# A mixture-of-experts trunk: the first half's conditional block moved ahead of its gate/up product, and two rooms refilled in quarters

## The chip, the cores and the metric

The kernel runs on one core of one Trainium2 chip. The metric is device time in microseconds; lower is better. The kernel before took 1186.21 us, the median of three runs (1185.47 to 1189.15). The engines are TensorE (PE), ScalarE (ACT), VectorE (DVE), GpSimd (POOL) and SyncE (SP, which here only issues transfers).

## The reference, cut to what matters

Two layers over 256 tokens of width 1024. Each layer is an attention with a residual (layer 0 differential attention, layer 1 latent attention), then a mixture of 64 experts in 8 groups; each token uses the best two experts of its best group.

```
for i in range(2):
    h = rms_norm(x, attn_norm[i])
    x = x + (diff_attention, mla_attention)[i](h, ...)
    h = rms_norm(x, ffn_norm[i])
    x = x + hier_moe(h, ...)

def hier_moe(t):                       # 256 tokens
    combine = ...                      # top group, then top 2 of its 8 experts; 256 x 64 weights
    for e in range(64):
        hid = silu(t @ w_gate[e]) * (t @ w_up[e])        # 1024 -> 256
        acc += combine[:, e, None] * (hid @ w_down[e])   # 256 -> 1024
```

All numbers are float32. Gate, up and down of one expert are 1 MB each, so each layer reads 192 MB of expert weights.

## The kernel before, in words

**Halves.** The experts are taken four at a time: 16 "halves" per layer, t = 0 to 15 (`for t in range(LAST + 1)` in `moe`). Each expert of a half has 32 slots for tokens, so a half is one 128-row tile. For each half: the tokens are gathered into the slots by a product with a 0/1 matrix (`Gather`, L1264, `sel`), gained into `xg` on DVE (L330), multiplied by gate and up of the four experts (`into`, `gate_up`, L1317: 32 matmuls for 8 blocks k of the width and four experts, in four column groups, two trace records each), activated and multiplied (`hidden_rows`: L1325 on ACT, L1327 on DVE), turned (L1335), multiplied by down (L1349), and added back to the token rows `xs` (L1389, L1354).

**Two paths.** If an expert of a half has more than 32 tokens, a second round of 32 slots (`second`) is run for that half. That is decided at run time: `ways` (step `fc`) counts tokens and writes a code `path` (L1242); `values_load` (L1482) loads it into a register of each engine at t = 0, and `full` (L1459) is an `If` on bit t. A further `If` within it (L1414) covers more than 64 tokens. All engines go through each such block. Each engine counts its finished work in a semaphore; at the end of the branch that was taken, an instruction per engine raises its count to a common value, so that what follows can wait for one number whichever way was gone. In the trace these are EVENT_SEMAPHORE at L1459.

**Weights.** Ten rooms of 2 MB in SBUF form a ring. A unit is gate and up of one expert, or down of two experts; unit n stands in the room that unit n - 10 left. `free` names the units whose room is done with, and issues on SP, in a fixed order, the loads that have become possible. In half t the gate/up units of its four experts are freed after the product (within `full`, as `done`, so once in each branch), and the two down units after the down product. Each load waits on SP for the last matmul that read its room. Completion of transfers is counted on eight semaphores in rotation, and a transfer also waits for the one eight before it.

**The start of a layer's experts.** The front of `moe` ends with the steps `FG10 FG11 fc fe0 fe1 fw0 fw1 fv`: the last two parts of the first gather (PE), `ways`, the two parts of `xg` (DVE), the weights of the tokens (L1188 to L1197, DVE and ACT), the weighted matrix (L1279, DVE) and the load of the activation table (ACT, L1115). In layer 0, 16 small DVE operations on the rope tables of layer 1 follow (L263 to L266). At t = 0 all ten rooms are full; experts 0, 1, 2 and 3 stand in rooms 0, 1, 2 and 3 in layer 0, in 9, 0, 1 and 4 in layer 1 (`RING`).

Of the kernel before, what the change touches and what calls it, by code (L numbers as in the profile page):

```python
# [54 lines left out]
ROOMS = 10  # L55
# [14 lines left out]
def trunk_kernel(  # L70
# [5 lines left out]
    nc = tc.nc  # L76
# [1211 lines left out]
    def moe(layer, front):  # L1288
# [6 lines left out]
        def free(units):  # L1295

            state["free"] = state["free"] | set(units)
            while order[state["next"]] - ROOMS in state["free"]:
                load_unit(layer, order[state["next"]])
                state["next"] += 1  # L1300

        def weights_of(g, e, n, part):
            return [front.d6 if (x, part) == (6, "d") else
                    half(expert_room(layer, x, part), x % 2) if part == "d" else rooms[expert_room(layer, x, part)]
                    for x in range(8 * g + e, 8 * g + e + n)]
# [62 lines left out]
        def into(t, j):  # L1368
            g, e, _ = halves_of(t)
            return gate_up(lambda k, at: xg[:, k, j, at], weights_of(g, e, 4, "g"))  # L1370
# [76 lines left out]
        state = {"next": 0, "free": set()}  # L1447
        def full(t, path, done):

            mark = dict(state)

            def at_once():

                state.update(mark)
                done()

            with tc.If((path >> t) & 1, preferred_fallthrough_block=True, label=f"full{layer}_{t}") as more:  # L1459
                second(t, at_once)  # L1460
            with more.Else():
                at_once()
                if t < LAST:
                    tc.mark_branch_hint_location(f"full{layer}_{t + 1}", "LikelyTaken", engines=[PE.engine])
# [5 lines left out]
        for t in range(LAST + 1):  # L1470
            g, _, pairs = halves_of(t)
            weight = None
            if t == LAST:
                back(ts, selT[:, (t + 1) % 2])

                weight = small("sums", 1)
                this.weighted(t, sel[:, (t + 1) % 2])
                DVE.tensor_reduce(weight, this.turned(sel[:, (t + 1) % 2]), axis=AX.XY, op=OP.add)
            gu = into(t, t % 2)
            hid = hidden_rows(gu, weight, held[0][:, 512:768])  # L1480
            if t == 0:
                path = nc.values_load(front.path[0:1, 0:1], min_val=0, max_val=2 ** 17 - 1)  # L1482
            full(t, path, lambda: free(units(g, pairs, "gu")))
            if t == LAST:
                rows = temp(256).bitcast(F32R).rearrange("p (b t) -> p b t", b=2)
                hdT = hidden_columns(hid)
# [99 lines left out]
```

## Time and profile before

| what | value |
|---|---|
| median of three runs | 1186.21 us (1185.47 to 1189.15) |
| the profiled execution | 1189.65 us, of which the span of the trace is 1187.9 us |
| PE busy | 970.6 us, 82% of the span |
| DVE, ACT busy | 425.8 us (36%), 232.0 us (20%) |
| mean granted TensorE clock | 0.935 of full speed |
| read from HBM | 433.03 MB |

The profile cuts the span into 40 slices of 29.7 us. Its GB/s line tells where the transfers run at their full pace (some 425) and where they don't; PE's idle time is listed by what ended it. Layer 0's experts begin at about 151 us, layer 1's at about 738 us; the starts of both are read closely below.

### The profile page before, as it was taken

The numbers are of one execution on the slowest core, as the hardware profiler recorded it, in microseconds if no ns is written. First come the engines' busy times: TensorE is split into PE (matmuls) and PEld (weight loads), VectorE is DVE, ScalarE is ACT, GpSimd is POOL, SyncE is SP. The second block draws the span as 40 slices with busy tenths as digits, with TensorE's granted clock in tenths as the row PEclk, the third lists the DMA queues.
The fourth block names the chain that finished last, engine by engine and source line by source line (L and its number), as shares of the span: only waits on it lengthen the run. The fifth ranks groups of instructions, "written<-read, shape, count | busy, mean of one in ns | idle before, by whom it ended". The sixth has DMA issues, their size and how long they took to land. (4 is left out here: it accounts for less than half of the span.)

```text
span 1187.9 us, 16711 instructions
## 1 busy us (share of the span) xinstructions
PE 970.6 (82%) x6544; PEld 544.0 (46%) x6544; DVE 425.8 (36%) x996; ACT 232.0 (20%) x594; POOL 1.3 (0%) x23
## 2 busy tenths in 40 slices
PE   8999888887776777777888999877777777789787
PEld 8897744433332333333448777533333333333343
DVE  6898633221111111111339886222111211113233
ACT  5666410000000000000017874100000000000001
POOL 0000000000000000000000000000000000000000
PEclk9999989998898889988999999989888988899999
DMA  9556968999999999999953387899999999999996
GB/s 353 203 210 261 353 255 363 383 425 426 425 425 425 426 425 425 426 426 426 412 220 141 136 311 300 354 426 425 426 426 426 426 425 426 425 424 378 424 426 263
DMA packets 78013, 435.97 MB, mean 367 GB/s; under 512 B 6960, under 2 KB 23088, under 8 KB 30128
## 3 DMA queue, kind: packets, MB, share of 16 engines
q1 hardware_dynamic: 77728, 434.02, 88.7%
q8 instruction: 86, 1.41, 0.4%
q14 instruction: 55, 0.45, 0.1%
q10 hardware_dynamic: 144, 0.09, 0.0%
HBM read 433.03 MB, written 1.05 MB: 365 GB/s over the span
## 5 line engine op out<-in xcount | busy, mean ns | idle before, releaser
L1317 PE MATMUL bank<-room,areaC 128*32 128x512 f32 x2240 | 332.0, 675 | 105.2 <-DMA room<-in_moe_w_up_dram 105.2
L1317 PEld LDWEIGHTS bank<-room,areaC 128*32 128x32 f32 x2240 | 97.0, 123 | 329.8 <-issue 314.5
L1327 DVE TENSOR_TENSOR prob<-temp,bank 128x256 f32<-128x256 f32 x33 | 13.9, 422 | 385.9 <-ACTq L1459 192.8
L1349 PE MATMUL bank<-room,aT 128*32 128x512 f32 (+1 forms) x1160 | 128.3, 572 | 1.2 <-ACT aT L1337 1.2
L1354 DVE TENSOR_TENSOR xs<-xs,bank 128x512 f32<-128x512 f32 (+1 forms) x148 | 96.9, 659 | 79.2 <-PE bank L1389 74.9
L1389 PE MATMUL bank<-prob,val 128*128 128x512 f32 x240 | 111.3, 607 | 3.1 <-issue 2.0
L1325 ACT ACTIVATE temp<-bank 128x256 f32<-128x256 f32 x35 | 13.4, 384 | 481.7 <-PE bank L1317 481.7
L418 PE MATMUL bank<-room,areaB 128*128 128x256 f32 (+3 forms) x544 | 87.9, 314 | 5.0 <-DVE room L386 2.8
L1264 PE MATMUL bank<-val,areaB 128*128 128x128 f32 x576 | 75.2, 292 | 18.8 <-DVE val L1256 15.2
L330 DVE TENSOR_TENSOR areaC<-bank,pack 128x512 f32<-128x512 f32 x70 | 48.4, 692 | 114.0 <-PE bank L1264 114.0
L1264 PEld LDWEIGHTS bank<-val,areaB 128*128 128x128 f32 x576 | 71.3, 205 | 24.6 <-DVE val L1256 17.4
L418 PEld LDWEIGHTS bank<-room,areaB 128*128 128x128 f32 x544 | 77.3, 194 | 10.0 <-DVE room L386 3.3
L1264 PE MATMUL bank<-val,areaA 128*128 128x128 f32 x544 | 66.9, 282 | 16.3 <-DVE val L1256 13.7
L1264 PEld LDWEIGHTS bank<-val,areaA 128*128 128x128 f32 x544 | 63.6, 196 | 20.5 <-DVE val L1256 17.3
L1389 PEld LDWEIGHTS bank<-prob,val 128*128 128x128 f32 x240 | 44.5, 196 | 50.6 <-issue 49.0
L1349 PEld LDWEIGHTS bank<-room,aT 128*32 128x32 f32 x1160 | 34.5, 109 | 67.4 <-issue 59.4
L386 DVE TENSOR_TENSOR room<-room,room 128x2048 fp32r<-128x2048 f32 (+4 forms) x33 | 62.4, 1898 | 4.3 <-ACT room L384 4.3
L1381 ACT COPY prob<-bank 128x512 f32<-128x512 f32 x30 | 17.6, 586 | 189.0 <-PE bank L1349 189.0
L384 ACT CAST room<-room 128x2048 fp32r<-128x2048 f32 (+4 forms) x33 | 51.8, 1590 | 5.2 <-DMA room<-in_diff_w_in_dram 2.7
L1381 DVE COPY prob<-bank 128x512 f32<-128x512 f32 x30 | 20.8, 692 | 89.4 <-PE bank L1349 89.4
L1285 PE MATMUL bank<-ident,val 128*128 128x128 f32 x74 | 15.5, 292 | 44.8 <-DVEq L1459 28.0
L418 PE MATMUL bank<-room,areaA 128*128 128x512 f32 (+1 forms) x176 | 42.9, 387 | 2.0 <-DVE areaA L688 2.0
(245 smaller groups left out, 734.5 us busy)
## 6 DMA issues: line engine op xcount, KB each, us to landing
room<-in_moe_w_gate_dram SPq DMA_DIRECT2D x124, 1024.0 KB, 19.5
room<-in_moe_w_up_dram SPq DMA_DIRECT2D x124, 1024.0 KB, 19.6
room<-in_moe_w_down_dram SPq DMA_DIRECT2D x122, 1024.0 KB, 19.6
room<-in_diff_w_in_dram SPq DMA_DIRECT2D x11, 1024.0 KB, 10.7
room<-in_diff_w_out_dram SPq DMA_DIRECT2D x2, 2048.0 KB, 9.4
room<-in_moe_w_gate_dram SPq DMA_DIRECT2D x8, 512.0 KB, 14.8
room<-in_moe_w_up_dram SPq DMA_DIRECT2D x8, 512.0 KB, 13.6
room<-in_moe_w_down_dram SPq DMA_DIRECT2D x8, 512.0 KB, 10.0
```

What stands on the lines that cost most here:

```text
L330: DVE.tensor_tensor(dst, tp, gain[:, k0:k0 + n, None].to_broadcast([128, n, dst.shape[2]]), op=OP.mult)
L384: step(c + name)(lambda f=f: f(hi().bitcast(F32R), w()))
L386: step(c + name)(lambda eng=eng: eng.tensor_tensor(lo().bitcast(F32R), w(), hi(), op=OP.subtract))
L418: PE.matmul(out, a[k][x_].bitcast(F32R), b[k][w_].bitcast(F32R), start=first and j == 0, stop=last and j == n - 1)
L1264: PE.matmul(self.ps[kk][:, k, :], self.front.xn[:, tb, 4 * kk + k, :], self.sel[:, tb, :], start=tb + k == 0, stop=tb == 1, skip_group_che ...
L1285: PE.transpose(tp[:, tb, :], (self.sel if sel is None else sel)[:, tb, :], ident)
L1317: PE.matmul(gu[M * c:M * c + M], x(k, slice(M * c, M * c + M)), w[:, :, k, :], start=k == 0, stop=k == 7)
L1327: DVE.tensor_mul(hid, sil, gu[:, 256:512])
L1349: PE.matmul(y[n][M * c:M * c + M], hdT[:, k, M * c:M * c + M], w[:, k, ns], start=first and k == 0, stop=last and k == 1, skip_group_check ...
L1354: DVE.tensor_add(xs[:, tb, ns], xs[:, tb, ns], acc)
L1381: (ACT.copy, DVE.tensor_copy)[n](t, y[n])
L1389: PE.matmul(acc, rows[:, tb, :], t, start=True, stop=True)
```

## The change

At t = 0 the `If` block stands ahead of the first gate/up product and no longer frees anything in its branches. The product follows it. Then `refill(4)` issues the loads that the freed rooms allow: gate and up of experts 7 and 9, which go to the rooms of experts 0 and 2, are cut into four parts along k (256 KB each, 2 KB per partition, where it was 1 MB and 8 KB), part by part for both experts; then down of 7, 8 and 9 in whole, into the rooms of experts 1 and 3. Bytes and rooms are the same. For t = 1 to 15 nothing changes but line numbers. (`load_expert` with `cuts` was there before.)

```
+        def refill(cuts):
+            for c in range(cuts):
+                for e in (7, 9):
+                    load_expert(layer, e, "gu", cuts, c)
+            for n in (ROOMS + 1, ROOMS + 4):
+                load_unit(layer, n)
+            state["next"] = 4
...
+            if t == 0:
+                path = nc.values_load(front.path[0:1, 0:1], min_val=0, max_val=2 ** 17 - 1)
+                full(t, path, lambda: None)
             gu = into(t, t % 2)
             hid = hidden_rows(gu, weight, held[0][:, 512:768])
             if t == 0:
-                path = nc.values_load(front.path[0:1, 0:1], min_val=0, max_val=2 ** 17 - 1)
-            full(t, path, lambda: free(units(g, pairs, "gu")))
+                refill(4)
+                free(units(g, pairs, "gu"))
+            else:
+                full(t, path, lambda: free(units(g, pairs, "gu")))
```

PE in layer 0 before, from the end of the first gather into the first product (rooms 0 to 3 carry numbers of their tiles: room_69, room_1590, room_1523 and room_72; names in brackets are the semaphores waited for, DVE_49 that of DVE, DMAHW those of transfers):

```order
L1264 MATMUL bank<-val,areaB 128x128 [waits DVE_49,Activation_49]
L1264 MATMUL bank<-val,areaB 128x128 x7
L1317 MATMUL bank<-room_69,areaC 32x512 [waits DMAHW1_49,DMAHW5_49,DMAHW0_49,DVE_49]
L1317 MATMUL bank<-room_1590,areaC 32x512 [waits DMAHW4_49,DMAHW3_49]
L1317 MATMUL bank<-room_1523,areaC 32x512 [waits DMAHW2_49,DMAHW1_49]
L1317 MATMUL bank<-room_72,areaC 32x512 [waits DMAHW7_49,DMAHW5_49]
L1317 MATMUL bank<-room_69,areaC 32x512 [waits DMAHW6_49]
```

The product stood right behind the gather; its wait for DVE is for the count that the first part of `xg` gives (302).

PE at the same place now, from the gather into the block:

```order
L1264 MATMUL bank<-val,areaB 128x128 [waits DVE_49,Activation_49]
L1264 MATMUL bank<-val,areaB 128x128 x7
L1490 TENSOR_LOAD path [waits DVE_49]
L1468 REGISTER_ALU
L1468 COMPARE_AND_BRANCH
L1596 BRANCH_PREFETCH_HINT
L1264 MATMUL bank<-val,areaB 128x128 [waits DVE_49,PE_49]
```

The load of `path` and the branch have moved between them; the last row is already the second round, which runs only if its bit is set.

PE now, from the end of the block into the first product:

```order
L1468 UNCONDITIONAL_BRANCH
L1596 BRANCH_PREFETCH_HINT
L1468 UNCONDITIONAL_BRANCH [waits PE_49]
L1326 MATMUL bank<-room_69,areaC 32x512 [waits DMAHW0_49,DMAHW1_49,DVE_49,DMAHW5_49,PE_49,Activation_49]
L1326 MATMUL bank<-room_1590,areaC 32x512 [waits DMAHW4_49,DMAHW3_49]
L1326 MATMUL bank<-room_1523,areaC 32x512 [waits DMAHW2_49,DMAHW1_49]
L1326 MATMUL bank<-room_72,areaC 32x512 [waits DMAHW7_49,DMAHW5_49]
L1326 MATMUL bank<-room_69,areaC 32x512 [waits DMAHW6_49]
```

The product's first matmul now waits for DVE, PE and ACT at once. In the built program the numbers are 354 for DVE and 168 for ACT; ahead of the block's end those counts reach 334 (with the last rope operation) and 150, and the block's end adds 28 and 20. In layer 1 it is 1254 for DVE, where 1238 is reached (with L1279) and 28 are added.

SP in layer 0 before, the loads in the branch that is taken when bit 0 is clear:

```order
L147 DMA room_69<-in_moe_w_gate_dram 128x2048 [waits DMAHW3_49,PE_49]
L147 DMA room_69<-in_moe_w_up_dram 128x2048 [waits DMAHW4_49]
L143 DMA room_1590<-in_moe_w_down_dram 128x2048 [waits DMAHW5_49,PE_49]
L147 DMA room_1523<-in_moe_w_gate_dram 128x2048 [waits DMAHW6_49,PE_49]
L147 DMA room_1523<-in_moe_w_up_dram 128x2048 [waits DMAHW7_49]
L143 DMA room_72<-in_moe_w_down_dram 128x2048 [waits DMAHW0_49,PE_49]
L143 DMA room_72<-in_moe_w_down_dram 128x2048 [waits DMAHW1_49]
```

Seven loads, each of the four rooms released by the last matmul that read it.

SP now, the first two of four parts, behind the block:

```order
L147 DMA room_69<-in_moe_w_gate_dram 128x512 [waits DMAHW3_49,PE_49]
L147 DMA room_69<-in_moe_w_up_dram 128x512 [waits DMAHW4_49]
L147 DMA room_1523<-in_moe_w_gate_dram 128x512 [waits DMAHW5_49,PE_49]
L147 DMA room_1523<-in_moe_w_up_dram 128x512 [waits DMAHW6_49]
L147 DMA room_69<-in_moe_w_gate_dram 128x512 [waits DMAHW7_49,PE_49]
L147 DMA room_69<-in_moe_w_up_dram 128x512 [waits DMAHW0_49]
L147 DMA room_1523<-in_moe_w_gate_dram 128x512 [waits DMAHW1_49,PE_49]
L147 DMA room_1523<-in_moe_w_up_dram 128x512 [waits DMAHW2_49]
```

Sixteen quarter loads and three whole ones stand here now; the first waits for the product's matmuls of k = 0 and 1 alone.

## Rows read from the trace of the kernel before

**Rows 1.** The page: GB/s in 40 slices; the costliest group of PE.

```profile
GB/s 353 203 210 261 353 255 363 383 425 426 425 425 425 426 425 425 426 426 426 412 220 141 136 311 300 354 426 425 426 426 426 426 425 426 425 424 378 424 426 263
...
L1317 PE MATMUL bank<-room,areaC 128*32 128x512 f32 x2240 | 332.0, 675 | 105.2 <-DMA room<-in_moe_w_up_dram 105.2
```

**Rows 2.** Stretches: us; PE, PEld, DVE, ACT, POOL busy; clock, DMA share, GB/s.

```profile
185.00:190.00 5.00, 5.00 (x52) 1.43 (x44) 0.00 (x0) 0.00 (x0) 0.00 (x0) 1.00 0.56 234
...
210.00:215.00 5.00, 5.00 (x52) 1.53 (x48) 1.33 (x3) 0.59 (x1) 0.00 (x0) 1.00 0.59 193
...
215.00:220.00 5.00, 5.00 (x48) 1.30 (x40) 0.00 (x0) 0.00 (x0) 0.00 (x0) 1.00 1.00 418
...
750.00:755.00 5.00, 5.00 (x49) 2.79 (x51) 1.38 (x2) 0.59 (x1) 0.00 (x0) 1.00 1.01 419
```

**Rows 3.** Timeline of layer 0's start: us from start, us taken, what; [idle before].

```profile
148.63 0.15 DVE L1242 CAST path<-temp 128x1 int32<-128x1 f32 x1
...
151.61 7.14 PE L1317 MATMUL bank<-room,areaC 128*32 128x512 f32 x64
...
157.84 0.18 DVE L266 SCALAR_TENSOR_TENSOR sin_t<-pack,pack 128x32 f32<-128x32 f32 x1
...
158.77 0.34 SPq L147 DMA_DIRECT2D room<-in_moe_w_gate_dram  x1
...
160.73 0.41 PE L1285 MATMUL bank<-ident,val 128*128 128x128 f32 x2 [1.98 <-PEq L1459]
...
167.76 3.64 PE L1349 MATMUL bank<-room,aT 128*32 128x512 f32 x32
```

**Rows 4.** Timeline of layer 1's start.

```profile
737.48 0.15 DVE L1242 CAST path<-temp 128x1 int32<-128x1 f32 x1
...
738.65 7.34 PE L1317 MATMUL bank<-room,areaC 128*32 128x512 f32 x64
...
743.01 0.42 DVE L1279 TENSOR_TENSOR val<-val,wt 128x256 f32<-128x256 f32 x1
...
745.74 0.34 SPq L147 DMA_DIRECT2D room<-in_moe_w_gate_dram  x1
```

**Rows 5.** Block at t = 0, layer 0: ns min/median/max, start in us.

```profile
L1459 PEldq COMPARE_BRANCH  x1: 3590/3590/3590, 156.7 to 156.7; - x1
L1482 PEldq TENSOR_LOAD <-path x1: 491/491/491, 156.0 to 156.0; - x1
L1459 DVEq EVENT_SEMAPHORE  x1: 21/21/21, 160.3 to 160.3; - x1
L1482 DVEq TENSOR_LOAD <-path x1: 541/541/541, 159.3 to 159.3; - x1
```

**Rows 6.** The same in layer 1.

```profile
L1459 PEldq COMPARE_BRANCH  x1: 3833/3833/3833, 743.5 to 743.5; - x1
L1482 PEldq TENSOR_LOAD <-path x1: 317/317/317, 743.0 to 743.0; - x1
L1459 DVEq EVENT_SEMAPHORE  x1: 21/21/21, 747.5 to 747.5; - x1
L1482 DVEq TENSOR_LOAD <-path x1: 322/322/322, 746.5 to 746.5; - x1
```

**Rows 7.** Who waited for instructions of L1459: us, times.

```profile
  PE bank L1285: 41.8, 28
```

**Rows 8.** Timeline of PE: the gate/up product behind waits of different lengths.

```profile
351.03 7.03 PE L1317 MATMUL bank<-room,areaC 128*32 128x512 f32 x58 [1.46 <-DMA room<-in_moe_w_up_dram]
...
781.32 4.50 PE L1317 MATMUL bank<-room,areaC 128*32 128x512 f32 x20 [3.84 <-DMA room<-in_moe_w_up_dram]
...
840.36 9.18 PE L1317 MATMUL bank<-room,areaC 128*32 128x512 f32 x58 [3.89 <-DMA room<-in_moe_w_up_dram]
```

**Rows 9.** Stretches: clock behind that wait; transfers in 1 KB pieces (layer 0's attention weights).

```profile
840.00:845.00 5.00, 4.64 (x24) 1.35 (x28) 0.00 (x0) 0.00 (x0) 0.00 (x0) 0.53 1.01 423
...
20.00:30.00 10.00, 10.00 (x86) 10.00 (x84) 8.09 (x34) 5.20 (x7) 0.00 (x0) 1.00 1.09 386
```

**Rows 10.** Timeline of PE: the gather behind a product with no block between.

```profile
179.64 3.84 PE L1264 MATMUL bank<-val,areaB 128*128 128x128 f32 x32 [1.37 <-DVE val L1256]
```

## The prediction

> **What bounds the kernel now.** I read the page first. Its GB/s line stands at about 425 through most of both expert stretches, and PE's largest idle time, 105.2 us at the gate/up product, is ended by transfers [rows 1]. So the experts are paced by the stream of weights, and what counts is when that stream starts and where it stops for want of a free room. Second, the stretches. In layer 0 the stream stops twice more after its start: it is busy for 0.56 of 185 to 190 us and 0.59 of 210 to 215, with PE busy for all of both; from 215 on it is full [rows 2]. Until about 213 us, layer 0 is therefore paced by PE, whose progress frees the rooms. In layer 1 the stream is full from 750 on, and its slices stay at 425 up to the one of 378 near the end [rows 1, 2]; PE comes to that later dip from waits for weights, so I take it to move with the stream. Third, the timelines of the two starts, for what the change moves [rows 3, 4], and the queue instructions of the block [rows 5, 6]. At t = 0 bit 0 is clear in both layers: the trace shows no second round between the first product and the first down product.
>
> This gives two gauges. Layer 0 ends later or earlier by the shift of PE, read at the first down product (now at 167.76, [rows 3]); when its first loads start matters little there, since the stream runs dry at 185 to 190 anyway. Layer 1 moves by the shift of its first load (now at 745.74, [rows 4]).
>
> **The wait that is added.** The first product used to wait for `xg` only. Behind the block it waits for a count that DVE reaches only at the block's end, and DVE gets there behind everything queued ahead: token weights, the weighted matrix and, in layer 0, the 16 rope operations. Before, these lay beside the product, which covered them; that cover is gone. That engines do wait for each other at the block's end is shown: 28 times, 41.8 us in all, PE's next transposes waited for instructions of L1459 [rows 7].
>
> When is DVE through? In layer 0 its last rope operation ends at 157.84 + 0.18 = 158.02, in layer 1 L1279 ends at 743.01 + 0.42 = 743.43 [rows 3, 4]. From the load of `path` to the instruction at the block's end it took 160.3 - 159.3 and 747.5 - 746.5, 1.0 us each [rows 5, 6]. Between nothing of that hidden and all of it, the end falls at 158.0 to 159.0 and 743.4 to 744.4. I let the load start with the last operation: 158.8 and 744.0, and 0.1 us more for PE to see it. The product then starts at 158.9 instead of 151.61, and at 744.1 instead of 738.65. Behind it on PE stand the gather and the first down product; ACT and DVE wait for its result, and SP, at the head of whose queue the refill stands, for its matmuls.
>
> PE's own way through the block is shorter and hidden: `path` is written at 148.78 and 737.63, and from PE's load to the end of its branch it took 156.7 + 3.59 - 156.0 = 4.3 us, and 4.3 in layer 1 [rows 3 to 6], so PE would be through at about 153.1 and 741.9. The Trainium skill ("Runtime: NRT & Kernel Launch", Instruction fetch mechanics) says that a taken branch whose target has not been fetched stalls the sequencer until it is; the 3.59 and 3.83 us of PE's branch agree. If that were all that the block costs here, the time would be that of the rival "PE's own branch" below.
>
> **The clock.** PE is then idle for 7.3 us in layer 0 and 5.5 in layer 1. Behind an idle time of 3.89 us the granted clock was 0.53 in 840 to 845, that is the 1.2 GHz level for nearly all of it, and 58 records of the product took 9.18 us; behind one of 1.46 us the same took 7.03 [rows 8, 9]. I add the difference, 2.15, to the product's 7.14: 9.3 us. Bounds: 7.14, if the clock holds, and 14.3 if it stayed low throughout.
>
> **Layer 0, summed at PE.** Behind the product the block is gone: 1.37 us to the gather, which takes 3.84 [rows 10]. The down product begins at 158.9 + 9.3 + 1.4 + 3.8 = 173.4, against 167.76: +5.7 us. Ends: 158.0 + 7.14 + 5.2 = 170.3, +2.6; 159.1 + 14.3 + 5.2 = 178.6, +10.9. The removed 1.98 us behind the product [rows 3] and whatever slowed the gather there before are in this sum. The loads of experts 7 and 9 start when k = 0 and 1 are done, some 3.6 us into a product at low clock (20 records in 4.50 us, 16 needed, [rows 8]): 162.5, against 158.77. They need 4.2 MB / 0.425 = 9.9 us plus a start of 1 to 2, so they are in by 174; the second product, 3.64 us behind 173.4, takes them at 177. Three microseconds hide them.
>
> **Layer 1, summed at the stream.** First load at 744.1 + 3.6 = 747.7, against 745.74: +2.0. Ends: 743.4 + 1.8 (a quarter of 7.14) = 745.2, -0.5; 744.5 + 3.6 = 748.1, +2.4. The stream then has 7 MB queued (17 us) and must get the two down rooms before 765; the first down product ends at 744.1 + 9.3 + 5.2 + 3.64 = 762.2, in time. Smaller pieces: 1 KB ones ran at 386 GB/s [rows 9], 8 KB ones at 425; 2 KB lie between, so the 4.2 MB cost 0 to 1.0 us more; I take 0.4. The issues are no bound: sixteen at 0.34 us [rows 3, 4] make 5.4 us for 9.9 us of transfer. In layer 0 both are hidden behind PE. Together +2.4.
>
> The Trainium skill ("DMA: Bandwidth & Descriptors", Bandwidth) advises at least 1 MiB per transfer and gives 341 GB/s for 1 MB alone and 138 for 64 KB; by the lower figure the 4.2 MB would take an estimated 30 us, 20 more. The trace has several transfers in flight and 386 GB/s in finer pieces, which speaks against it here.
>
> **Sum.** +5.7 + 2.4 = +8.1 us on the profiled execution (1189.65 us, span 1187.9). That lies 3.4 above the median, without a sign that the two starts differ, so I put the sum on the median: 1186.2 + 8.1 = 1194.3.
>
> **The rivals.**
> 1. *The clock holds* (the idle time falls so that the low level is short): 158.9 + 7.14 + 5.2 - 167.76 = +3.5, and 744.1 + 1.8 - 745.74 = +0.2; 1189.9. For it: behind 1.46 us nothing was lost [rows 8], and the low level ends by itself once PE is busy. Against it: idle times here are longer than the 3.89 that brought the low level.
> 2. *PE's own branch is the only price*, the other side: if the product started at 153.1 and 741.9, layer 0 would be 153.1 + 7.14 + 5.2 - 167.76 = -2.3, layer 1 741.9 + 1.8 - 745.74 + 0.4 = -1.6; 1182.3, faster by 0.33%. It decides if DVE is through the block before 155 and 743. Against it: DVE's rows end at 158.0 and 743.4, and the wait is in PE's rows of the change. Only if the count were met earlier than I read it does this hold.
> 3. *Layer 0's delay is taken up by the stream*: if the loads, not PE, set 213 us, only layer 1's +2.4 is left; 1188.6. For it: 2 us of stream idle at 210 to 215. Against it: that idle time is ended by PE's progress.
> 4. *Quarters starve the stream*: at half the pace the 4.2 MB take 9.9 us more in layer 1, and in layer 0 the second product waits some 7 us: 1211. Against it: the 386 GB/s.
>
> **Chances.** The forecast 0.70 (its own range 1191 to 1198: the block's end by 0.5 us, the clock by 2 us, in both layers); the clock holds 0.13; PE's own branch 0.05; taken up 0.07; quarters 0.05. About 0.3%, 3.6 us, is what a measurement of this kernel can tell from no change: 1182.7 to 1189.8. Rival 1 lies on that edge and is halved. Slower: 0.70 + 0.07 + 0.05 = 0.82; same: 0.06 + 0.07 = 0.13; faster 0.05. The range 1188.5 to 1198.5 leaves out the quarters, PE's own branch and the far end of the clock.
>
> **What would show it.** In the profile after: the first product at about 159 in layer 0 and 744 in layer 1, with PE's idle time before it of 7 and 5.5 us, ended by DVE's or PE's queue at L1468; a clock near half in its first microseconds; the first quarter load at 162 and 747.5; the first down product at 173; then the gap of the stream at 190 to 196 and 216 to 219, as before but 5 to 6 later. A first product at 153 would make me wrong, and so would a layer 0 that reaches full stream at 215 in spite of a late down product.

## The result, and the profile after

The changed kernel takes 1206.4 us (median of 6 runs, 1204.21 to 1210.59); the kernel before took 1188.36 beside it (6 runs, 1185.47 to 1189.52). The ratio is 1.0153, with a 95% interval of 1.0137 to 1.0170: 18 us slower, where 8.1 had been forecast. The profiled execution has a span of 1204.2 us, 16.3 more than the one of before. In this kernel the block's lines are L1468 and L1490, the product L1326, the gather still L1264, the down product L1358.

The page, in the lines that answer to [rows 1]: the stream is paced as before, and PE's idle time ahead of the product has grown from 105.2 to 121.2 us, of which transfers ended 109.0.

```profile
GB/s 354 195 234 255 326 226 266 383 426 426 424 426 425 426 426 426 425 425 426 416 254 141 126 311 297 297 425 425 426 426 425 426 426 426 425 422 360 424 424 258
...
L1326 PE MATMUL bank<-room,areaC 128*32 128x512 f32 x2240 | 330.7, 675 | 121.2 <-DMA room<-in_moe_w_up_dram 109.0
```

The other 12.2 stand in the view of who waited for instructions of L1468 (us, times; answers to [rows 7]): two waits of the product, one in each layer, that the kernel before did not have.

```profile
  PE bank L1326: 12.2, 2
```

Layer 0's start, in the timeline (start, duration, what, idle before; answers to [rows 3, 10]):

```profile
147.81 0.15 DVE L1242 CAST path<-temp 128x1 int32<-128x1 f32 x1
...
157.01 0.19 DVE L266 SCALAR_TENSOR_TENSOR sin_t<-pack,pack 128x32 f32<-128x32 f32 x1
157.47 9.17 PE L1326 MATMUL bank<-room,areaC 128*32 128x512 f32 x64 [6.61 <-DVEq L1468]
161.09 0.34 SPq L147 DMA_DIRECT2D room<-in_moe_w_gate_dram  x1
...
171.79 3.64 PE L1358 MATMUL bank<-room,aT 128*32 128x512 f32 x32
```

Layer 1's start in the same view (answers to [rows 4]):

```profile
746.44 2.02 PE L1264 MATMUL bank<-val,areaA 128*128 128x128 f32 x16 [0.73 <-DVE temp L1237]
...
747.22 0.15 DVE L1242 CAST path<-temp 128x1 int32<-128x1 f32 x1
...
754.05 9.57 PE L1326 MATMUL bank<-room,areaC 128*32 128x512 f32 x64 [5.59 <-DVEq L1468]
757.67 0.34 SPq L147 DMA_DIRECT2D room<-in_moe_w_gate_dram  x1
```

And the block's own instructions in layer 0, as [rows 5] showed them (ns, then start in us):

```profile
L1468 PEldq COMPARE_BRANCH  x1: 3561/3561/3561, 148.8 to 148.8; - x1
L1468 DVEq EVENT_SEMAPHORE  x1: 21/21/21, 157.2 to 157.2; - x1
```

All this is what the prediction described. PE is through its branch at 152.4, and the product waits until DVE, behind its last rope operation, is at the block's end; it then takes 9.2 and 9.6 us, and 155 to 160 us has a granted clock of 0.50 (below), the 1.2 GHz level. What the prediction did not have comes later, on PE, in the second half of the experts (t = 1), which in layer 0 takes a second round (gather, product). Its first product ran as before, from 175.24 for 7.05 us; then:

```profile
183.76 1.80 PE L1264 MATMUL bank<-val,areaB 128*128 128x128 f32 x14 [1.46 <-DVE val L1256]
189.58 4.00 PE L1264 MATMUL bank<-val,areaB 128*128 128x128 f32 x18 [4.02 <-issue]
193.51 8.05 PE L1326 MATMUL bank<-room,areaC 128*32 128x512 f32 x64
```

Before, the same gather ran in one piece of 3.84 us ([rows 10]) and the product behind it took 7.07 from 183.40. Now PE stops for 4.02 us after 14 of the 32 matmuls, waiting for nothing that the profile shows ("issue"), and then runs the rest at a low clock (0.50 in 190 to 195 us). The gather ends 6.0 us later behind its start than before, the product takes 1.0 us more: 7.0 us together. The stretches show what it does to the stream of weights (PE, PEld, DVE, ACT, POOL busy; clock, DMA share, GB/s; answers to [rows 2]):

```profile
155.00:160.00 5.00, 2.53 (x12) 1.67 (x16) 2.17 (x18) 0.22 (x1) 0.00 (x0) 0.50 0.00 0
...
190.00:195.00 5.00, 5.00 (x25) 3.69 (x28) 1.72 (x3) 0.00 (x0) 0.00 (x0) 0.50 0.37 157
195.00:200.00 5.00, 5.00 (x48) 1.40 (x44) 0.00 (x0) 0.00 (x0) 0.00 (x0) 0.95 0.00 0
200.00:205.00 5.00, 3.23 (x32) 1.10 (x28) 0.42 (x1) 1.03 (x3) 0.00 (x0) 1.00 0.51 159
220.00:225.00 5.00, 5.00 (x50) 1.89 (x52) 1.26 (x2) 0.59 (x1) 0.00 (x0) 1.00 0.61 252
```

Before, at the first stop of the stream, the transfers were busy for 0.56 of one slice (185 to 190) and 0.72 of the next; now for 0.37, nothing and 0.51 of three (190 to 205).

**Where the 16.3 us are.** I summed the GB/s column over stretches of 2 us, in this trace and in that of before, and compared the times at which the same number of bytes had arrived. Bytes are counted from 140 us of each execution on, so that its lead or lag at that time is taken out (the changed kernel's was 0.9 us ahead there); the span is as it is. The table (us later than before; every kernel's single profiled execution) is used for the experiments too. Executions differ by themselves: e10, which leaves layer 0 as it was before, shows -1.4 there, so a difference of 1 to 2 us in one cell proves nothing. 10 MB lies at 177 us of the kernel before, 40 at 255, 210 at 718 (just ahead of layer 1's experts), 240 at 802, 370 at 1111.

| kernel | 10 MB | 40 MB | 210 MB | 240 MB | 370 MB | span |
|---|---|---|---|---|---|---|
| changed | +5.0 | +12.0 | +10.7 | +15.2 | +16.6 | +16.3 |
| e1, no hint in layer 0 | +6.1 | +5.0 | +4.1 | +11.5 | +13.1 | +17.5 |
| e2, hint later | +4.4 | +10.8 | +10.3 | +16.9 | +16.3 | +16.6 |
| e3, whole loads | +7.5 | +11.1 | +10.9 | +21.0 | +22.0 | +23.8 |
| e4, block behind the product | +6.3 | +0.6 | +0.3 | +6.8 | +9.3 | +10.0 |
| e5, DVE early | +1.4 | +7.5 | +6.7 | +8.2 | +8.9 | +9.3 |
| e6, e1 and e5 | +0.9 | +0.7 | -0.1 | +1.6 | +1.9 | +2.5 |
| e7, quarters inside the block | -2.9 | +3.4 | +2.8 | +1.1 | +1.9 | +1.2 |
| e8, halves inside the block | -2.2 | +3.9 | +2.9 | +1.7 | +2.5 | +1.5 |
| e9, PE filled | +7.7 | +6.7 | +13.2 | +23.3 | +24.9 | +26.1 |
| e10, quarters in layer 1 | -1.4 | -1.5 | -1.4 | -3.0 | -1.9 | 0.0 |
| e11, e10 without the hint | -1.5 | -0.1 | 0.0 | -2.7 | -3.4 | -4.0 |
| e12, e9 less one hint | +8.7 | +6.4 | +6.8 | +14.3 | +15.1 | +14.5 |
| e13, quarters backward | +10.4 | +18.2 | +17.3 | +30.0 | +29.7 | +29.9 |

For the changed kernel: 5.0 us for the late first product, 7.0 for the idle time at t = 1 and the low clock behind it, 1.3 given back in the rest of layer 0 and in layer 1's attention, 4.5 at the start of layer 1's experts, 1.4 in layer 1's late stretch; the 1.3 and the 1.4 are no larger than what executions differ by. Of the 4.5, the first load gives little over 2 (it is 11.93 us later than before, `path` 9.74) and the quarters' slow arrival the rest, 2.3.

### The profile page after: what moved, and what is told of

Same layout as the page of the kernel before. It is cut to its first block, busy times and chain, and to the rows that moved or that the text cites. A ratio compares the mean times of both kernels' runs of the same rounds, so it can differ in the third digit from the quotient of the medians.

```text
span 1204.2 us, 16755 instructions
## 1 busy us (share of the span) xinstructions
PE 968.8 (80%) x6544; PEld 544.4 (45%) x6544; DVE 425.3 (35%) x996; ACT 232.0 (19%) x594; POOL 1.3 (0%) x23
## 5 line engine op out<-in xcount | busy, mean ns | idle before, releaser
L1326 PE MATMUL bank<-room,areaC 128*32 128x512 f32 x2240 | 330.7, 675 | 121.2 <-DMA room<-in_moe_w_up_dram 109.0
L1326 PEld LDWEIGHTS bank<-room,areaC 128*32 128x32 f32 x2240 | 99.1, 123 | 342.6 <-issue 327.1
L1358 PE MATMUL bank<-room,aT 128*32 128x512 f32 (+1 forms) x1160 | 128.3, 572 | 1.2 <-ACT aT L1346 1.2
L1264 PE MATMUL bank<-val,areaB 128*128 128x128 f32 x576 | 75.6, 293 | 21.8 <-DVE val L1256 15.1
L1264 PEld LDWEIGHTS bank<-val,areaB 128*128 128x128 f32 x576 | 71.7, 206 | 27.7 <-DVE val L1256 15.1
L1264 PE MATMUL bank<-val,areaA 128*128 128x128 f32 x544 | 66.8, 282 | 16.4 <-DVE val L1256 13.7
L1264 PEld LDWEIGHTS bank<-val,areaA 128*128 128x128 f32 x544 | 63.5, 195 | 20.6 <-DVE val L1256 17.3
L1358 PEld LDWEIGHTS bank<-room,aT 128*32 128x32 f32 x1160 | 34.5, 109 | 67.4 <-issue 59.4
L1285 PE MATMUL bank<-ident,val 128*128 128x128 f32 x74 | 15.1, 285 | 42.0 <-DVEq L1468 26.6
## 6 DMA issues: line engine op xcount, KB each, us to landing
room<-in_diff_w_in_dram SPq DMA_DIRECT2D x11, 1024.0 KB, 10.7
```

Source lines behind the costliest of these rows:

```text
L1264: PE.matmul(self.ps[kk][:, k, :], self.front.xn[:, tb, 4 * kk + k, :], self.sel[:, tb, :], start=tb + k == 0, stop=tb == 1, skip_group_che ...
L1285: PE.transpose(tp[:, tb, :], (self.sel if sel is None else sel)[:, tb, :], ident)
L1326: PE.matmul(gu[M * c:M * c + M], x(k, slice(M * c, M * c + M)), w[:, :, k, :], start=k == 0, stop=k == 7)
L1358: PE.matmul(y[n][M * c:M * c + M], hdT[:, k, M * c:M * c + M], w[:, k, ns], start=first and k == 0, stop=last and k == 1, skip_group_check ...
```

## The experiments

The theories: the late first product costs what the prediction said, and (1) the idle time at t = 1 comes from the branch hint that PE executes as it leaves the block, or from the place of the code, or from both; (2) quarters arrive slowly, by themselves or because of the product beside them. Ratios are to the kernel before, run beside each.

### The hint of the second half (e1, e2)

In the block's `Else`, PE executes a hint that the next half's block will be jumped over. In layer 0 that is wrong for t = 1, which falls through into its second round. e1 leaves this one hint out:

```
             with more.Else():
                 at_once()
-                if t < LAST:
+                if t < LAST and t + layer:
                     tc.mark_branch_hint_location(f"full{layer}_{t + 1}", "LikelyTaken", engines=[PE.engine])
```

> The changed kernel, less one instruction of PE in layer 0: the branch hint for the block of the second half (t=1) that PE executes as it leaves the block of the first half. Theory A (the hint stands in the way of the code that follows in line): the 4.0 us idle in the gather of the second half's second round (14 matmuls, idle, 18 matmuls, at 185.6 to 189.6 us) goes, the clock holds, the product behind it takes 7 instead of 8 us and starts near 187.5 instead of 193.5; the stream's stop at 195 to 200 us goes; time 1206.4 - 7 = 1199.5 us (1198 to 1201). Rival B (the place of the code: the same idle comes from where the moved instructions end a piece of code that is loaded as one): the idle stays where it is, time 1206 us (1205 to 1208). Rival C: the idle goes, but the stream takes the 7 us back before the end of layer 0, time 1206 us with no gap in the trace.

Measured: 1203.18 us, ratio 1.0113 (1.0098 to 1.0128). PE's timeline of it, against the rows of the changed kernel above, and at the end of the front of layer 1:

```profile
184.26 3.81 PE L1264 MATMUL bank<-val,areaB 128*128 128x128 f32 x32 [1.46 <-DVE val L1256]
188.00 7.07 PE L1326 MATMUL bank<-room,areaC 128*32 128x512 f32 x64
...
740.72 3.75 PE L1264 MATMUL bank<-val,areaA 128*128 128x128 f32 x16 [0.73 <-DVE temp L1237]
...
750.05 10.07 PE L1326 MATMUL bank<-room,areaC 128*32 128x512 f32 x64 [5.58 <-DVEq L1468]
```

The idle time is gone, and layer 0's stream is 7.0 us earlier at 40 MB, as A said; C is out. The whole gained some 5 us by the ratios (1.0153 less 1.0113), not 7, and the time missed A's bound of 1201. Where the rest went is not shown. The profiled execution is the slowest of the four (1207.22 us; the others took 1202.37 to 1203.63) and slower than the changed kernel's: its last gather ahead of layer 1's product ran for 3.75 us where that took 2.02, its stream lost 7.4 us there instead of 4.5, and some 4 more behind 370 MB.

e2 gives the hint, but behind the first product:

```
-                if t < LAST:
+                if 0 < t < LAST:
                     tc.mark_branch_hint_location(f"full{layer}_{t + 1}", ...)
...
             if t == 0:
+                tc.mark_branch_hint_location(f"full{layer}_1", "LikelyTaken", engines=[PE.engine])
                 refill(4)
```

> The changed kernel with the branch hint for the second half's block moved from the end of the first block, ahead of the first product, to behind that product, in both layers, as it stands in the order of the kernel before. The run without the hint in layer 0 lost the 4.0 us idle there, so the hint takes part in it. Theory A (what matters is that the hint comes 131 PE instructions ahead of where it was): the idle goes, the time is that of the run without the hint, ratio 1.011 (1203 us). Rival B (the hint does it wherever it stands, together with where the code ends): the 4 us idle stays in the second round's gather, ratio 1.015 (1206 to 1208 us).

Measured: 1210.29 us, ratio 1.0185 (1.0165 to 1.0204). The gather again stops after 14 matmuls: rival B.

```profile
189.10 4.00 PE L1264 MATMUL bank<-val,areaB 128*128 128x128 f32 x18 [4.05 <-issue]
```

So it isn't the order of hint and product, which the kernel before had like this, too. What differs from before is then where the code lies, or when PE comes to it; the runs below speak for the place.

### The code moved by 96 instructions (e9, e12)

e9 puts 48 small matmuls on PE between the block and the first product; they also tell what the low clock costs.

```
                 full(t, path, lambda: None)
+                idle = psum_bank()
+                for _ in range(48):
+                    PE.matmul(idle[:, 0:128], ones_b, ones_b, start=True, stop=True)
             gu = into(t, t % 2)
```

> The changed kernel with 48 dummy matmuls of 128 columns (as the ones that the kernel has at its start) on PE between the block and the first product, in both layers, where PE waits for DVE. They move PE's code behind them by 96 instructions and keep PE busy. Clock (theory A: the product is slow because PE was idle): the first product takes 7.1 to 7.6 us in place of 9.2 to 9.6, starting when it did, layer 1's stream 1.5 us earlier. Code (theory A: 4 us idle comes with the hint wherever a piece of code ends): the idle moves 96 instructions ahead, into the second half's first product, and stays 4 us. Rival B: the place of the code matters too and the idle goes. Time: 1.0153 - 0.002 - 0.001 = 1.012 to 1.013 (1204 us) with the idle kept, 1.007 (1198 us) without it.

Measured: 1213.57 us, ratio 1.0201 (1.0166 to 1.0235). PE's timeline, start and the two second rounds of layer 0:

```profile
156.06 4.62 PE L1494 MATMUL bank<-ones_b 128*128 128x128 bf16 x48 [6.55 <-DVEq L1468]
160.61 7.07 PE L1326 MATMUL bank<-room,areaC 128*32 128x512 f32 x64
...
184.88 3.81 PE L1264 MATMUL bank<-val,areaB 128*128 128x128 f32 x32 [1.46 <-DVE val L1256]
188.62 7.07 PE L1326 MATMUL bank<-room,areaC 128*32 128x512 f32 x64
...
601.69 1.47 PE L1264 MATMUL bank<-val,areaB 128*128 128x128 f32 x11 [1.42 <-DVE val L1256]
607.61 4.85 PE L1264 MATMUL bank<-val,areaB 128*128 128x128 f32 x21 [4.45 <-issue]
```

Three things follow. The dummies waited for DVE's end of the block themselves (the same label, 6.55 us) and so came on top of it, which I had not foreseen; the time says nothing of the clock's worth. But the product behind the busy dummies took 7.07 us instead of 9.17, at a granted clock of 1.00 in 160 to 165 us (0.52 in 155 to 160, where the dummies ran): the 2.1 us were the idle time's. And the stop at t = 1 is gone with its hint in place, while the other second round of layer 0, that of t = 15, has one that neither kernel had: 4.45 us, and 6.5 us lost in the stream between 40 and 210 MB. The expectation's theory A had the stop move into the first product of t = 1; it did not, so that form of the theory falls.

e12 is e9 less the hint for t = 15 in layer 0:

```
-                if t < LAST:
+                if t < LAST and (layer or t != 14):
```

> The run with 48 dummy matmuls lost the 4 us idle at the second half's second round, and got 4.45 us of idle in the gather of the other second round that layer 0 takes, that of the last half (11 matmuls, idle, 21 matmuls, at 603.2 to 607.6 us). Here that run's kernel less the one hint for the last half's block in layer 0. Theory A (a hint for a block that is not jumped over, and a piece of code that ends soon behind it, make the idle): the 4.45 us go, with 0.7 us of slower product behind, ratio 1.0201 - 0.005 = 1.015. Rival B (the idle there belongs to the dummies' shift of the code alone): it stays, ratio 1.020.

Measured: 1206.49 us, ratio 1.0149 (1.0134 to 1.0164), as A had it. The gather of t = 15 in PE's timeline:

```profile
602.15 3.81 PE L1264 MATMUL bank<-val,areaB 128*128 128x128 f32 x32 [1.42 <-DVE val L1256]
605.89 7.07 PE L1326 MATMUL bank<-room,areaC 128*32 128x512 f32 x64
```

So in two places a stop of 4.0 to 4.5 us needed both: a hint for a block that then fell through, and the code at that place. It is the place and not the moment: in e5 below PE comes to this gather 4.5 us earlier and stops behind the same 14 matmuls. What points at code being fetched are the transfers of the changed kernel in 187.0 to 187.5 us, half a microsecond within the stop (queue, packets, MB, share of 16 engines):

```profile
q1 hardware_dynamic: 27, 0.19, 89.3%
q8 instruction: 1, 0.02, 12.0%
```

One packet of 0.02 MB of instructions lies in it, between weights that fill the engines. In 146 to 196 us the changed kernel has four such packets (near 149.5, 153, 172.5, 187), e1 five. Read in steps of 0.1 us, every stop of this kind has one (changed, e2, e3, e5, e9, e13, and the shorter stops within a gather of the kernel before, e4, e10 and e11), and PE goes on 2.2 to 2.5 us behind it. But e1 has a packet at the same point of the gather, 3.5 us behind its start, and no stop, so a packet alone doesn't make one. That the hint takes the place of the piece that follows in line is the reading that fits; which piece each packet brought the trace does not say, so this mechanism is argued, and only the parts of the hint and of the place are shown.

The Trainium skill ("Runtime: NRT & Kernel Launch", Instruction fetch mechanics) calls the prefetch purely sequential and names the taken branch as what breaks it. Here the stop stood behind a branch that was not taken, but hinted as taken (4.02 us, none without the hint); the page has no such case.

### DVE's work behind the product (e5), and with e1 (e6)

e5 leaves ahead of the block only what ACT's exponentials need; the rest of the token weights, the weighted matrix and the rope tables come behind the first product.

```
-            step("fv")(lambda: (self.first.weighted(0), ACT.preload_act_table_set("silu_and_others")))
+            step("fv")(lambda: ACT.preload_act_table_set("silu_and_others"))
...
             ACT.activation(e2, d, AF.Exp)
+
+        def weights_end(self, tb):
             DVE.scalar_tensor_tensor(se, e2, 1.0, sg, op0=OP.add, op1=OP.mult)
...
             gu = into(t, t % 2)
+            if t == 0:
+                for tb in range(2):
+                    front.weights_end(tb)
+                this.weighted(0)
+                if layer == 0:
+                    for tb in range(2):
+                        rope_tables(1, tb)
```

> The changed kernel with DVE's work on the token weights (behind their exponentials), the weighted rows and the rope tables put behind the first product in the program, so that DVE comes to the end of the block some 4.5 us earlier in layer 0 and 3.4 us in layer 1. Theory A (the product waits for DVE's queue at the end of the block, as its idle of 6.61 and 5.59 us is labelled): product of layer 0 starts at 153.0 instead of 157.5 and of layer 1 3.4 us earlier after the path (3.4 instead of 6.8 us behind it); if PE's clock holds over the shorter wait each takes 7.2 instead of 9.2 to 9.6 us. Layer 1's first load comes 4 to 5 us earlier behind the path. Time 1206.4 - 4.4 - 4.4 = 1197.6 us (1195 to 1201) with the idle at the second round staying. Rival B (PE itself, by its taken branch, is what comes last): product starts within 1 us of where it did, time 1206 us.

Measured: 1201.22 us, ratio 1.0100 (1.0083 to 1.0117). The timeline, both layers:

```profile
148.22 0.15 DVE L1246 CAST path<-temp 128x1 int32<-128x1 f32 x1
...
153.30 8.82 PE L1328 MATMUL bank<-room,areaC 128*32 128x512 f32 x64 [3.75 <-DVE wt L1201]
...
743.34 0.15 DVE L1246 CAST path<-temp 128x1 int32<-128x1 f32 x1
...
748.21 7.74 PE L1328 MATMUL bank<-room,areaC 128*32 128x512 f32 x64 [1.90 <-DVE sums L1198]
750.12 0.33 SPq L147 DMA_DIRECT2D room<-in_moe_w_gate_dram  x1
```

The product now starts 5.1 and 4.9 us behind `path` instead of 9.7 and 6.8, 0.6 us behind the end of PE's own branch in both: A, in the mechanism. It gained some 6 us where I had 8.8: the product stayed slow in layer 0 (8.82 us where I had 7.2), and layer 1's first load came 3.7 us earlier behind `path`, not 4 to 5. The stop at t = 1 stayed (4.02 us).

e6 is e1 and e5 together.

> The changed kernel with both repairs: no hint for the second half in layer 0, and DVE's work on the weights, weighted rows and rope tables behind the first product. If the two costs are separate (theory A) their gains add: ratio 1.0153 - 0.0040 - 0.0053 = 1.006, 1196.5 us (1194.5 to 1198.5), with layer 0 less than 2 us behind the kernel before and the rest lost at layer 1's start (quarters). Rival B (one stands behind the other, the stream takes it up): ratio 1.009 to 1.010, 1200 us or more.

Measured: 1194.6 us, ratio 1.0056 (1.0040 to 1.0072): the gains add, as A had it. Layer 0 is level with before (+0.7 us at 40 MB). So the two costs are separate, and together nearly all that layer 0 lost.

### The quarters (e3, e4, e7, e8, e13)

e3 refills in whole loads, `refill(1)` for `refill(4)`.

> The changed kernel with the two rooms refilled by four whole loads in place of sixteen quarters. A whole load must wait for the last matmul on its room, so layer 1's first load starts near 763.7 us instead of 757.7 (+6.0). Theory A (the quarters' start-up costs 2.3 us: 0.96 MB short at 0.41 MB/us in the first 8 us): the stream is whole within 2 us of its start, net +3.7 us, time 1210 us (1209 to 1211.5). Rival B (the slow start comes from something else, the quarters cost nothing): +6.0 us, 1212.4 us. Rival C (the quarters cost as much as they bring): 1206.4 us.

Measured: 1211.88 us, ratio 1.0184 (1.0170 to 1.0199), 3.7 us over the changed kernel by the ratios, which is A's figure. Transfers in layer 1, by stretches of 2 us (last column GB/s), first of e3, whose product ended at 766.4, then of the changed kernel, whose quarters start at 757.7:

```profile
766.00:768.00 2.00, 1.39 (x10) 0.76 (x7) 0.76 (x2) 0.84 (x3) 0.00 (x0) 1.00 0.47 70
768.00:770.00 2.00, 2.00 (x20) 2.00 (x20) 0.15 (x1) 0.28 (x1) 0.00 (x0) 1.00 1.00 418
```

```profile
758.00:760.00 2.00, 2.00 (x20) 1.44 (x16) 0.00 (x0) 0.00 (x0) 0.00 (x0) 0.81 0.54 147
760.00:762.00 2.00, 2.00 (x24) 1.48 (x20) 0.00 (x0) 0.00 (x0) 0.00 (x0) 1.00 0.84 277
762.00:764.00 2.00, 1.99 (x18) 0.81 (x10) 0.00 (x0) 0.29 (x1) 0.00 (x0) 1.00 1.03 296
764.00:766.00 2.00, 1.40 (x11) 1.32 (x12) 0.76 (x2) 0.83 (x3) 0.00 (x0) 1.00 0.93 295
766.00:768.00 2.00, 2.00 (x20) 2.00 (x19) 0.69 (x1) 0.00 (x0) 0.00 (x0) 1.00 1.02 375
```

Whole loads are at 418 GB/s two microseconds after the first one; quarters stay at 277 to 296 for six, with the engines' share at 0.84 to 1.03, so hardly for want of work: the transfers themselves take longer. From first load to steady stream the changed kernel lost 2.4 us and e3 nothing (shift at 240 MB, here with the bytes of the whole execution counted, 14.3 and 20.4 us, less the shift of the first load, 11.9 and 20.4). The expectations have 0.6 for whole loads and 3.2 to 4.0 for quarters; those figures set the table's shift, counted from 140 us, against a first load that is not, and so are too large by the lead at 140 us.

e13 turns the quarters' order round, so that the first waits for the end of the product and none has it beside it.

```
-            for c in range(cuts):
+            for c in reversed(range(cuts)):
```

> The changed kernel with the quarters of both rooms issued in the opposite order, the last two k steps' quarter first: it must wait for the end of the product, and then all the others may follow at once, with no product beside them. First load near 763.7 us in layer 1 (path 747.2 + 16.5) instead of 757.7. Theory A (quarters are slow by themselves, through their short pieces): 3 to 3.6 us of start-up again, GB/s near 290 for the first 4 MB, net +6.0 us, ratio 1.020. Rival B (they are slow because each waits for its k steps, or because they run beside the product): 420 GB/s at once, start-up 0.6 us as with whole loads, net +3.4 us, ratio 1.018 as with whole loads.

Measured: 1219.57 us, ratio 1.0226 (1.0193 to 1.0260). First load at 773.07, as the product ends:

```profile
774.00:776.00 2.00, 1.79 (x14) 1.71 (x15) 0.49 (x2) 0.44 (x2) 0.00 (x0) 1.00 0.83 199
776.00:778.00 2.00, 2.00 (x20) 2.00 (x20) 0.69 (x1) 0.00 (x0) 0.00 (x0) 1.00 0.92 243
778.00:780.00 2.00, 2.00 (x20) 0.80 (x23) 0.69 (x1) 0.00 (x0) 0.00 (x0) 1.00 0.99 297
780.00:782.00 2.00, 2.00 (x23) 0.64 (x18) 0.00 (x0) 0.59 (x1) 0.00 (x0) 1.00 1.02 384
```

Slow again, without the product and without waits for its steps: A, as far as the rate goes. A's reason, the short pieces, is not shown. The 1 KB pieces of [rows 9] came in loads of 1 MB, and those were at 372 GB/s in 4 to 6 us of the kernel before, 3 to 5 us behind their first issue; and halves (e8 below), with pieces of 4 KB, were at 293 and 266 GB/s in 744 to 748 us of layer 1, while they were being issued, and at 399 behind that, once all eight were. So it goes with the size of a load, or with how much is under way (a load also waits for the one eight before it, so no more than eight quarters, 2 MB, are out at a time); no run tells these two apart. (The profiled execution is beyond A's 1.020, since the whole wait also came back in layer 0: its second product waited 3.98 us for a late quarter. The six times lie between 1208.47 and 1221.31 us, so the median says little.) The Trainium skill ("DMA: Bandwidth & Descriptors", Bandwidth) advises transfers of at least 1 MiB; the prediction had weighed that and set it aside, and 290 against 418 GB/s agrees with the advice; its 138 is for 64 KB alone, which no run here has.

e4 puts the block back behind the product and issues the quarters behind it.

```
-            if t == 0:
-                path = nc.values_load(front.path[0:1, 0:1], min_val=0, max_val=2 ** 17 - 1)
-                full(t, path, lambda: None)
             gu = into(t, t % 2)
             hid = hidden_rows(gu, weight, held[0][:, 512:768])
             if t == 0:
+                path = nc.values_load(front.path[0:1, 0:1], min_val=0, max_val=2 ** 17 - 1)
+                full(t, path, lambda: None)
                 refill(4)
```

> The kernel before with the block where it was, behind the first product, and the two rooms refilled in quarters as in the changed kernel, outside the block. Theory A: SP passes the block as soon as the path is written (737.5 us in layer 1), so the first quarter starts once the first two of the eight k steps have been multiplied, 738.65 + 1.85 + 0.2 = 740.7 us instead of 745.74 (-5.0); the quarters' start-up gives back 2.3; layer 0 is paced by PE there and gains 0; PE's code stands as in the kernel before and has no new idle time: 1188.4 - 2.7 = 1185.7 us (1184 to 1187). Rival B (the quarters' start-up eats all): 1188.4 us (same). Rival C (the idle in the second half's second round comes from the quarters or from SP being past the block early, not from PE's order): 4 us idle there, 1193 us or more.

Measured: 1197.42 us, ratio 1.0057 (1.0039 to 1.0075); none of the three (C's time, but not its idle, which is 0.76 us). SP's queue in 735 to 775 us (waited for; us in total, times, longest):

```profile
SPq L147 <- PEq L1468: 8.9, 1, 8.9
```

Behind a block a load waits for PE's end of the block, as the product waits for DVE's: first load 748.52, later than the 745.74 of [rows 4]. I had taken into account only that SP itself passes early.

e7 issues the quarters inside the block, in place of the whole loads, at t = 0 of the kernel before; e8 halves, `refill(2)`.

```
-            full(t, path, lambda: free(units(g, pairs, "gu")))
+                full(t, path, lambda: (refill(4), free(units(g, pairs, "gu"))))
```

> The kernel before with the quarters of the two rooms issued inside its block, where the whole loads stand: PE's, DVE's and ACT's order is untouched. The run with the quarters behind the block had its first load wait for PE's end of the block (748.5 us); inside it they wait for the product's steps alone. Theory A: layer 1's first load comes 4.5 to 5 us earlier (740.7 to 741.3 instead of 745.74 us), the quarters' start-up (3.2 to 4.0 us in the runs so far, 0.6 with whole loads) gives most of it back: net -1.2 us, ratio 0.999 (0.997 to 1.001). Rival B (the quarters are slow only because the product is slow beside them): net -4.5 us, ratio 0.996. Rival C (quarters in flight are cut short by the number of loads that can be under way, and cost more the earlier they start): ratio 1.002 or more.

> As the run with the quarters in the block of the kernel before, with halves (eight loads of 512 KB) in their place. The first load waits for four of the eight k steps: 738.65 + 3.7 + 0.2 = 742.5 us (-3.2). Theory A (what the start-up costs goes with the number of loads and the length of their pieces, half as many and twice as long): start-up 1.5 us, net -1.7 us, ratio 0.9985 (0.997 to 1.000). Rival B (the start-up cost is the same as with quarters): net +0.5 us, ratio 1.0005.

Measured: e7 1191.01 us, ratio 1.0017 (1.0004 to 1.0030); e8 1192.14 us, 1.0033 (1.0020 to 1.0045). The first load of e7 in layer 1 starts when expected:

```profile
738.92 7.34 PE L1326 MATMUL bank<-room,areaC 128*32 128x512 f32 x64
740.86 0.34 SPq L147 DMA_DIRECT2D room<-in_moe_w_gate_dram  x1
```

So it is 4.9 us earlier than before; the stream kept 1.7 of it (from +2.8 to +1.1). In layer 0 both runs lost 3 to 4 us by 40 MB, which I had not expected: the stream that had run ahead by 2 to 3 us stopped at PE's pace all the same, and PE itself was slower there. The trace shows where: PE's branch into the `Else`, in e7's layers 0 and 1, then in e10's layer 0, which has no quarters.

```profile
L1468 PEldq COMPARE_BRANCH  x1: 6331/6331/6331, 153.4 to 153.4; - x1
L1468 PEldq COMPARE_BRANCH  x1: 6655/6655/6655, 743.8 to 743.8; - x1
L1468 PEldq COMPARE_BRANCH  x1: 3331/3331/3331, 154.9 to 154.9; - x1
```

Where no load is under way beside it, the branch takes 3.3 to 3.9 us ([rows 5, 6], the changed kernel and the other runs whose loads start behind the block, layer 0 of e10 and e11); beside the early loads 5.9 to 7.6 (both layers of e7 and e8, layer 1 of e10 and e11). PE's idle time behind it was 4.47 us in layer 0 of e7, 1.98 before ([rows 3]), and the clock was at 0.50 in the five microseconds that followed. Loads that start early enough to run beside PE's branch thus cost PE 2 to 4 us; that the code is fetched behind the weights is the likely reason, which no run tests. Halves were no better than quarters.

### Two candidates against the kernel before (e10, e11)

e10 is e7 with the quarters in layer 1 alone; e11 is e10 without the hint of e1.

```
+                full(t, path, lambda: (refill(4) if layer else None, free(units(g, pairs, "gu"))))
```

> The kernel before with quarters inside the block in layer 1 alone; layer 0 as before. From the run with them in both layers: its stream in layer 1 went from +2.7 to +1.0 us against the kernel before, so the quarters there bring 1.7 us, and its layer 0 lost 2.7 to 3.4 us. Theory A (the two layers are separate): ratio 0.9986, 1187.4 us (1186 to 1189). Rival B (layer 0's loss in that run was PE's clock by chance): ratio 0.998 to 1.000, not to be told apart from A by time, by the stream's shift in layer 0 alone.

> As the run before it in this list, less the hint for the second half in layer 0. In the kernel before PE stood idle 0.99 us in the first half's gather, labelled issue. Theory A (that idle comes from the hint as well): it goes, layer 0 is 1 us earlier, ratio 0.9978, 1186.4 us (1185 to 1188). Rival B (that idle is the code behind a taken branch that has not come yet, with or without a hint): it stays, ratio as in the run with the hint.

Measured: e10 1189.45 us, ratio 0.9997 (0.9980 to 1.0014); e11 1187.64 us, 0.9986 (0.9967 to 1.0004). Neither is shown to be faster than before; both beat the changed kernel by 18 to 20 us, by the ratios. Layer 0's loss is gone in e10, and its stream keeps 1.6 us at layer 1's start, as A had it, but they don't show in the time. The idle time in the first half's gather, 0.99 us before, is 2.55 us in e10 and 2.39 in e11: it is there with or without the hint. That much of rival B is shown; that it is code which has not come yet is argued from where it lies, soon behind the block's taken branch.

## Why the prediction was wrong

- **The wait that is added**: right. Product at 157.47 and 754.05, idle 6.61 and 5.59 us ended by DVE's queue at L1468, forecast 7.3 and 5.5. Behind `path` that is 9.66 and 6.83 us; forecast 10.3 and 6.6 ([rows 3, 4]). e5, which took DVE's work out of the way, moved the product to PE's own branch.
- **The clock**: right. 9.17 and 9.57 us against 9.3, with 7.07 behind busy dummies.
- **Layer 0, summed at PE**: right as far as it went. The first down product came 4.03 us later than in [rows 3], 4.8 behind a `path` that was 0.8 earlier; forecast 5.7.
- **The step that failed** is the one that let this shift stand for the whole of layer 0 ("Layer 0 ends later or earlier by the shift of PE, read at the first down product"). It took PE's rows behind the first product as fixed. They were not: the moved code brought a stop of 4.02 us and a slow clock into t = 1. It was wrong by 7 us, the stop and what the low clock took behind it; without the hint (e1) both were gone. The rows that could have warned were there, the branch of 3.59 us in [rows 5], and in the code a hint for a block that falls through; the prediction used the first for the block alone and did not ask where else code would be fetched.
- **Layer 1, first load**: the size was right: +2.2 behind `path`, forecast +2.0.
- **Layer 1, quarters**: the term was mis-sized: 0.4 forecast, 2.4 measured (none with whole loads, e3). The bound was taken from 386 GB/s in finer pieces [rows 9]; but those came in loads of 1 MB, and a short piece in a large load says little of a small load. Rival 4 named the mechanism, at four times its size in layer 1 (9.9 us) and with a chance of 0.05.
- **Of the rivals**, 1 to 3 fell; the late wait was not taken up by the stream, but 1.3 us of layer 0's delay came back before layer 1's experts.

With +5.0, +7.0, -1.3, +4.5 and +1.4 the sum is 16.6, at the profile's 16.3 (of which some 0.9 less lies ahead of 140 us and 0.5 more behind 370 MB). The two shifts that the prediction added up, 5.0 and 2.2 us as measured, are near its 5.7 and 2.0, and e5 shows their cause, so that part was no luck.

## What to carry to other kernels

A conditional block cost not only its branch here: what came behind it waited until another engine had reached its end, the product 6.61 and 5.59 us for DVE, a load 8.9 us for PE. So look first at what is queued on that engine ahead of the block. When code moves, look at each block that is hinted one way and goes the other: a stop of 4 us can come up or vanish far from the edit, and it should be priced as a chance. Cutting a load to start it earlier pays only what the smaller loads don't lose: in e7 3 of 5 us went back, and PE's branch, with the earlier loads beside it, took 2.8 us longer.

## What the runs showed of the hardware

- With a hint for a jump that was then not taken, PE stopped for 4.0 to 4.5 us in the code behind the branch and ran slow behind the stop: 6.5 to 7 us in all. Leaving the hint out removed it in both places tried; moving the code by 96 instructions moved it from one place to the other.
- PE's taken branch at t = 0 took 3.3 to 3.9 us with no load under way, 5.9 to 7.6 beside loads.
- Sixteen loads of 256 KB on one queue came at 199 to 297 GB/s for six microseconds at their start, with the engines' share at 0.83 to 1.03, four loads of 1 MB at 418 after two.
- 48 small matmuls, 4.6 us of work right ahead of it, had the product run at a granted clock of 1.00: 7.07 us, where it took 9.17 behind idle time.
